# A longer latency for GpSimd's two-column power in the scheduler of a 256-token encoder trunk

## The chip, the cores and the metric

The kernel runs on one core of a Trainium2 chip. The metric is the time of one execution on the device in microseconds (us); of several executions the median is taken. The engines are TensorE (PE for its matmuls, PEld for its weight loads), VectorE (DVE), ScalarE (ACT), GpSimd (POOL) and the queue that issues the transfers (SP).

## What is computed

The trunk has two layers of width 1024 over 256 tokens, in float32. Each layer is a half-step feed-forward block, a mixer, and a second half-step feed-forward block. The mixer of the first layer is recurrent (a causal convolution, then a gated linear recurrence); the mixer of the second is differential attention on keys and values that are built once from the output of the first layer.

```python
def rmsnorm(x, g, eps=EPS):
    y = x * lax.rsqrt(jnp.mean(x * x, axis=-1, keepdims=True) + eps)
    return y * g

def swiglu(h, w_gate, w_up, w_down):
    return (jax.nn.silu(h @ w_gate) * (h @ w_up)) @ w_down

for layer in range(DEPTH):                      # DEPTH = 2
    if layer == N_A_LAYERS:                     # N_A_LAYERS = 1
        k_shared, v_shared = shared_kv(x, ...)
    x = x + 0.5 * swiglu(rmsnorm(x, ffn1_norm[layer]), ...)      # d_ff = 2816
    h = rmsnorm(x, mix_norm[layer])
    x = x + (recurrent_block(h, ...) if layer < N_A_LAYERS else diff_attention(h, k_shared, v_shared, ...))
    x = x + 0.5 * swiglu(rmsnorm(x, ffn2_norm[layer]), ...)
```

## The kernel before, in words

**Layout.** The activations stand transposed: channels on the 128 partitions, the 256 tokens along the row, so x is eight tiles of 128 x 256. Weights come in blocks of 128 x 128, eight to a granule of 128 x 1024. Every float32 weight is split into two parts of a shorter type: ScalarE casts the high part (`whi<-raw`), VectorE subtracts it and keeps the low part (`wlo<-raw,whi`). The activations are split in the same way (`xs` for a normalised input, `b` for a product inside a block). A product is then made of a matmul with the high weights against 512 columns (high and low activations side by side) and one with the low weights against 256 columns (`mm2`), or of three matmuls of 256 columns (`mm3`, in the mixers).

**The norm factor.** A norm's gain is put into `xs` beforehand, its factor per token is applied after the product. `rstd` makes it: two matmuls of the squares against a column of ones (`aux<-ones,acc`), one VectorE instruction (`rv`), a power of -0.5 on the two columns of `rv` by GpSimd (`rt_f`, `rt_mix` or `rt_l`), two VectorE instructions that lay the factor on a diagonal (`w<-ident,rt_f`), one float32 matmul that spreads the diagonal over all rows (`aux<-w,ones`, two records in the trace: "the spread"), and a copy by ScalarE into `rb`. VectorE multiplies the products by `rb` later. `rstd` is called six times: "f10", "f20", "l1" and "f21" for the four feed-forward blocks, "mix0" for the recurrent mixer, and "mix1" for attention, which uses the factor per partition and makes no spread.

**What sets the order.** All operations are first recorded (`Recorder.add`), each with a pitch (how long its engine is taken) and a latency (after how long its result can be used) from the function `cost`. `Recorder.plan` then places them one by one on the five engines: at each step it takes the operation that can start first by these estimates, and among those that can start within 60 ns of each other the one with the longest tail of work behind it. The order found in this way, and the buffer of each tile, are then emitted as they are; on the chip an engine takes its instructions in this order and waits at the head of its queue for what is missing. A later estimate for a result therefore moves whatever waits for it further back in its engine's queue, and other work forward.

**Names in the trace.** All instructions are emitted from line 385 and so carry the line L385; they are told apart by the tiles. `mm` is one of six PSUM banks for products, `aux` one of two for everything else. `w` are working tiles. In the feed-forward blocks `w<-mm,w` adds the two halves of a product, which frees the bank, and `w<-w,rb` applies the norm factor. In the recurrent mixer `rbuf<-mm,rb` frees the bank and applies the factor in one, and the small block products of the gates take `w` (a split activation) and `xk` (their weights).

Of the kernel before, what the change touches and what calls it, by code (L numbers as in the profile page):

```python
# [101 lines left out]
def is_ap(v):  # L102
    return hasattr(v, "tensor") and hasattr(v, "ap")


def width(v):
    n = 1
    for _, c in v.ap[1:]:
        n *= c
    return n  # L110
# [12 lines left out]
def sources(a, k):  # L123
    vals = list(a if "out" in k else a[1:]) + [v for n, v in k.items() if n not in ("out", "accum_out")]
    return [v for v in vals if is_ap(v)]


def cost(op):
    k, out = op.k, op.outs[0] if op.outs else None
    ins = sources(op.a, k)  # L130
    psum = [v for v in ins if v.space == bass.MemoryType.PSUM]
    n = width(out) if out is not None else 1
    if op.eng == "tensor":
        if op.fn == "transpose":
            return 109, 220
        m = width(k["rhs"])
        if k["rhs"].dtype == BF16:
            return m / 2.4 + 3, m / 2.4 + 175
        if k["rhs"].dtype == F32R:
            return 0.4428 * m + 3.3, 0.4428 * m + 165  # L140
        p = 4 * m / 2.4 + 3 if m > 8 else 222
        if k["lhsT"].ap[0][1] <= HD:
            p /= 2
        return p, p + 170
    if op.eng == "scalar":
        if op.fn == "preload_act_table":
            return 1294, 1283
        scalars = is_ap(k.get("scale")) + is_ap(k.get("bias"))
        p = n / 1.2 + (65 if psum else 100) + 83 * scalars
        lat = n / 1.2 + (172 if psum else 195) + 93 * scalars  # L150
        return (p + 93, lat + 200) if len(op.outs) > 1 else (p, lat)
    if op.eng == "vector":
        if op.fn in ("reduce_sum", "reduce_max"):
            n = width(ins[0])
        if op.fn == "tensor_copy":
            return n / 1.92 + 67, n / 1.92 + 155
        if op.fn == "memset":
            return max(15, n / 0.96 - 60), n / 0.96 + 40
        if op.fn == "tensor_tensor_scan":
            return n * 2 / 0.96 + 55, n * 2 / 0.96 + 140  # L160
        rate = 0.96
        if op.fn == "tensor_scalar" and not psum:
            rate = 1.92
        scalar = op.fn in ("tensor_scalar", "scalar_tensor_tensor") and len(ins) > (1 if op.fn == "tensor_scalar" else 2)
        return n / rate + (125 if scalar else 68), n / rate + (210 if scalar else 153)
    if op.eng == "gpsimd":
        if op.fn == "memset":
            return 30, 100
        if k.get("op") == ALU.pow:
            return 300 + 170 * n, 340 + 170 * n  # L170
        return 120 + 2.14 * n, 160 + 2.14 * n
    return 420, 0


class Recorder:
# [16 lines left out]
    def add(self, eng, fn, a, k):  # L192
# [3 lines left out]
        op.outs = [v for v in ([k["out"]] if "out" in k else list(a[:1])) + [k.get("accum_out")] if is_ap(v)]  # L196
        ins = sources(a, k)
        op.pitch, op.lat = cost(op)
        op.port = False
        op.narrow = eng == "tensor" and fn == "matmul" and k["lhsT"].ap[0][1] <= HD  # L200
# [974 lines left out]
```

## Time and profile before

| what | value |
|---|---|
| runs before | 935.24, 938.60, 938.62 us, median 938.60 |
| the profiled execution | 935.45 us, of which the span of its instructions is 933.7 us |
| PE busy | 927.1 us (99%) |
| PEld busy | 823.4 us (88%) |
| DVE busy | 723.1 us (77%) |
| ACT busy | 579.8 us (62%) |
| POOL busy | 34.0 us (4%) |
| granted TensorE clock | full (2.4 GHz) through the span |

The span is the time from the first to the last instruction on the engines; 1.75 us of the execution lie around it. A matmul's end is modelled, so that two matmuls that follow each other closely overlap in the rows; how fast TensorE goes is read from the distance between their starts. In the rows, a bracket with "idle before <- releaser" says how long the engine stood idle before the instruction and what ended that.

By stages: 0 to 195 us is the first feed-forward block (start-up to about 22), 195 to 267 the recurrent mixer, 267 to 462 and 462 to 646 two feed-forward blocks, 646 to 740 keys, queries, values and attention, then the last feed-forward block to 933.7.

### The profile page before, as it was taken

To read this page: it belongs to the slowest core of one execution; us is meant where nothing else is said; L and a number is where in the kernel's file an instruction comes from. 1 tells how busy PE (TensorE), PEld (TensorE's weight loads), DVE (VectorE), ACT (ScalarE), POOL (GpSimd) and SP (SyncE) were. 2 spreads that over 40 slices of the span, in tenths; PEclk is the share of its full clock that TensorE was granted. 3 is DMA by queue.
4 is the path that set the end of the run, shared out by engine and by line. 5 is a ranking of instruction groups with operands and counts; after the bars stand their busy time and mean duration, and the time that the engine had idled before them with its cause. 6 is when DMAs were issued, how large, how long until landed. Compare 5 with 4: busy or idle time off the path is not lost.

```text
span 933.7 us, 14664 instructions
## 1 busy us (share of the span) xinstructions
PE 927.1 (99%) x5586; PEld 823.4 (88%) x5586; DVE 723.1 (77%) x1229; ACT 579.8 (62%) x1040; POOL 34.0 (4%) x42
## 2 busy tenths in 40 slices
PE   8999999999999999999999999999999999999998
PEld 6888888899998888888888888888878988888887
DVE  7898887679898888866688788666997688888651
ACT  7666565569975565655565656555589865655541
POOL 0200000000000000000000000001220000000000
PEclk9999999999999999999999999999999999999999
DMA  9665556543475555555555555555443555555540
GB/s 314 247 210 196 181 183 232 208 145 135 139 264 185 181 184 194 200 189 181 187 180 200 200 181 181 191 201 193 143 147 122 177 180 181 183 192 202 201 155 18
DMA packets 25991, 172.33 MB, mean 185 GB/s; under 512 B 3136, under 2 KB 4288, under 8 KB 5568
## 3 DMA queue, kind: packets, MB, share of 16 engines
q1 hardware_dynamic: 25920, 171.39, 53.2%
q8 instruction: 44, 0.72, 0.3%
q14 instruction: 27, 0.22, 0.1%
HBM read 170.33 MB, written 1.05 MB: 184 GB/s over the span
## 4 chain that ended last, share of the span: by engine, by line
PE 93%; DVE 3%; POOL 1%; DMA 1%; issue 1%; SPq 0%; ACT 0%; DVEq 0%; ACTq 0%; POOLq 0%
PE mm L385 91%; PE aux L385 2%; DVE w L385 1%; DMA raw<-wts 1%; DVE wlo L385 1%; DVE ss L385 0%; SPq L385 0%; POOL facq L385 0%; POOL fac L385 0%; POOL rt_mix L385 0%; POOL rt_f L385 0%; DVE acc L385 0%; ACT w L385 0%; DVE fac L385 0%; DVE xs L385 0%
## 5 line engine op out<-in xcount | busy, mean ns | idle before, releaser
L385 PE MATMUL mm<-xs,whi 128*128 128x512 f32 (+1 forms) x1632 | 530.0, 377 | 1.1 <-DVE xs L385 0.9
L385 DVE TENSOR_TENSOR wlo<-raw,whi 128x1024 fp32r<-128x1024 f32 x318 | 388.4, 1224 | 124.1 <-ACT whi L385 123.6
L385 ACT CAST whi<-raw 128x1024 fp32r<-128x1024 f32 x318 | 333.1, 1051 | 198.3 <-PE mm L385 176.3
L385 PE MATMUL mm<-xs,wlo 128*128 128x256 f32 x1520 | 425.7, 281 | 0.1
L385 PEld LDWEIGHTS mm<-xs,whi 128*128 128x128 f32 x1632 | 298.1, 188 | 59.8 <-ACT acc L385 0.7
L385 PE MATMUL mm<-b,whi 128*128 128x512 f32 (+1 forms) x982 | 292.2, 359 | 0.0
L385 PEld LDWEIGHTS mm<-xs,wlo 128*128 128x128 f32 x1520 | 287.1, 189 | 0.8 <-DVE wlo L385 0.5
L385 PE MATMUL mm<-b,wlo 128*128 128x256 f32 x832 | 233.0, 281 | 0.0
L385 PEld LDWEIGHTS mm<-b,whi 128*128 128x128 f32 x982 | 174.6, 188 | 28.6 <-issue 0.3
L385 PEld LDWEIGHTS mm<-b,wlo 128*128 128x128 f32 x832 | 157.5, 189 | 0.0
L385 ACT ACTIVATE w<-mm 128x256 f32<-128x256 f32 x207 | 79.2, 384 | 110.0 <-PE mm L385 105.2
L385 DVE TENSOR_TENSOR w<-mm,w 128x256 f32<-128x256 f32 x176 | 73.2, 420 | 27.2 <-ACT w L385 27.1
L385 DVE TENSOR_TENSOR w<-w,rb 128x512 f32<-128x512 f32 x88 | 60.4, 689 | 0.4
L385 DVE TENSOR_TENSOR w<-w,w 128x256 f32<-128x256 f32 (+2 forms) x104 | 45.2, 439 | 0.0
L385 PE MATMUL mm<-whi,xk 128*128 128x512 f32 x128 | 41.3, 396 | 0.0
L385 ACT ACTIVATE w<-w 128x256 f32<-128x256 f32 x88 | 36.5, 418 | 5.7 <-DVE w L385 4.9
L385 ACT CAST b<-w 128x256 fp32r<-128x256 f32 x88 | 35.4, 406 | 4.1 <-DVE w L385 4.0
L385 DVE TENSOR_TENSOR b<-w,b 128x256 fp32r<-128x256 f32 x88 | 36.3, 417 | 1.9 <-ACT b L385 1.9
L385 DVE SCALAR_TENSOR_TENSOR xa<-mm,xa 128x256 f32<-128x256 f32 x32 | 13.5, 423 | 26.6 <-PE mm L385 18.6
L385 PEld LDWEIGHTS mm<-whi,xk 128*128 128x128 f32 x128 | 23.8, 188 | 4.6
L385 PE MATMUL mm<-wlo,xk 128*128 128x512 f32 x64 | 25.1, 393 | 0.0
L385 ACT ACTIVATE xs<-xa,vt 128x256 fp32r<-128x256 f32 x40 | 19.5, 502 | 7.3 <-DVE xa L385 7.3
(127 smaller groups left out, 494.0 us busy)
## 6 DMA issues: line engine op xcount, KB each, us to landing
raw<-wts SPq DMA_DIRECT2D x159, 1024.0 KB, 4.8
xa<-head SPq DMA_DIRECT2D x4, 256.0 KB, 5.4
raw<-wts SPq DMA_DIRECT2D x2, 512.0 KB, 7.9
outT<-xa SPq DMA_DIRECT2D x8, 128.0 KB, 2.2
xa<-head SPq DMA_DIRECT2D x2, 384.0 KB, 5.2
rw<-rows SPq DMA_DIRECT2D x1, 320.0 KB, 6.2
xa<-head SPq DMA_DIRECT2D x1, 260.0 KB, 3.6
ident<-eye SPq DMA_DIRECT2D x1, 64.0 KB, 9.9
```

The lines of the kernel that those rows point to most:

```text
L385: getattr(getattr(self.nc, op.eng), op.fn)(*op.a, **op.k)
```

## The change

One constant: the latency that `cost` gives to a power on GpSimd is 900 ns longer where the result has at most two columns (340 + 340 + 900 = 1580 ns instead of 680 ns). No instruction is added or taken away.

```diff
         if k.get("op") == ALU.pow:
-            return 300 + 170 * n, 340 + 170 * n
+            return 300 + 170 * n, 340 + 170 * n + (900 if n <= 2 else 0)
```

Powers on two columns are the six of `rstd` and one in the first block's set-up. GpSimd and SP issue the same rows in the same order as before. TensorE, VectorE and ScalarE have the same instructions in another order at a few places.

TensorE at the first norm factor ("f10"); `mm_152` and `mm_153` are the third column of the gate and up products, `aux_139` is the spread:

```order
 L385 MATMUL mm_153<-xs_0_86,whi_102 128x512
-L385 MATMUL aux_139<-w_7_138,ones_80 128x256
 L385 MATMUL mm_153<-xs_0_86,wlo_103 128x256
 L385 MATMUL mm_152<-xs_0_87,whi_133 128x512
+L385 MATMUL mm_153<-xs_0_87,whi_133 128x512
+L385 MATMUL aux_139<-w_7_138,ones_80 128x256
 L385 MATMUL mm_152<-xs_0_87,wlo_134 128x256
-L385 MATMUL mm_153<-xs_0_87,whi_133 128x512
 L385 MATMUL mm_153<-xs_0_87,wlo_134 128x256
```

The spread stands behind three more matmuls: one of 256 columns and two of 512.

VectorE at the same place; `w_0_141` is the first gate and up product, whose banks `mm_129` and `mm_130` it empties:

```order
 L385 TENSOR_SCALAR rv_136<-aux_135 128x2
 L385 TENSOR_TENSOR wlo_156<-raw_154,whi_155 128x1024
-L385 TENSOR_SCALAR w_7_138<-ident_79,rt_f_0_137 128x128 x2
 L385 TENSOR_TENSOR w_0_141<-mm_129,w_8_142 128x256
 L385 TENSOR_TENSOR w_0_141<-mm_130,w_9_143 128x256
+L385 TENSOR_SCALAR w_7_138<-ident_79,rt_f_0_137 128x128 x2
 L385 TENSOR_TENSOR wlo_158<-raw_154,whi_157 128x1024
```

The two instructions for the diagonal stand behind the two that empty the banks. At "f20", "l1" and "f21" the same happens in small: the diagonal stands behind one such instruction, the spread behind one matmul of 256 and one of 512 columns more. At "mix0" the spread stands behind two more matmuls of 256 columns.

In the recurrent mixer the later factor rearranges the work behind it. The largest move on TensorE is that of the last gate product, `aux_573`, whose input is the split activation `w_5_561`:

```order
 L385 MATMUL mm_578<-xs_0_126,whi_564 128x256 x2
 L385 MATMUL mm_578<-xs_0_126,wlo_565 128x256
+L385 MATMUL aux_573<-w_5_561,xk_459 128x256
 L385 MATMUL mm_578<-xs_0_127,whi_564 128x256 x2
 L385 MATMUL mm_578<-xs_0_127,wlo_565 128x256
-L385 MATMUL mm_578<-xs_0_128,whi_564 128x256 x2
+L385 MATMUL mm_578<-xs_0_128,whi_564 128x256
+L385 MATMUL aux_573<-w_5_561,xk_459 128x256 x5
+L385 MATMUL mm_578<-xs_0_128,whi_564 128x256
 L385 MATMUL mm_578<-xs_0_128,wlo_565 128x256
```

Its first matmul stood behind 7 matmuls of `mm_578` and now stands behind 18; its other five stood behind 11 and now stand behind 22.

ScalarE makes the high part of that activation (`CAST w_5_561`):

```order
 L385 ACT_TABLE_LOAD
-L385 CAST w_5_561<-w_9_560 128x256
 L385 ACTIVATE b_0_494<-b_0_494 128x1024
+L385 CAST w_5_561<-w_4_560 128x256
 L385 ACT_TABLE_LOAD
```

The cast stands behind the square root over 1024 columns, no longer ahead of it.

In attention TensorE and VectorE keep their order. ScalarE, before; `rt_mix_0_1454` is the factor of "mix1", `aux_1464` holds transposed queries:

```order
L385 COPY b_0_1380<-aux_1459 128x4x128
L385 ACTIVATE w_2_1455<-mm_1440,rt_mix_0_1454 128x512
L385 ACTIVATE w_5_1460<-mm_1441,rt_mix_0_1454 128x512
L385 COPY b_0_1380<-aux_1464 128x4x128
L385 CAST whi_1511<-raw_1508 128x1024
```

Now the copy out of `aux_1464` stands ahead of the two squares that need the factor:

```order
L385 COPY b_0_1380<-aux_1459 128x4x128
L385 COPY b_0_1380<-aux_1464 128x4x128
L385 ACTIVATE w_2_1455<-mm_1440,rt_mix_0_1454 128x512
L385 ACTIVATE w_5_1460<-mm_1441,rt_mix_0_1454 128x512
L385 CAST whi_1511<-raw_1508 128x1024
```

At the end of the recurrent mixer some products of its output change places with each other on TensorE, and VectorE adds two output tiles to x ahead of one weight split instead of behind it.

## Rows read from the trace of the kernel before

**Rows 1.** The page, part 1: busy time, share of the span, instructions of each engine.

```profile
PE 927.1 (99%) x5586; PEld 823.4 (88%) x5586; DVE 723.1 (77%) x1229; ACT 579.8 (62%) x1040; POOL 34.0 (4%) x42
```

**Rows 2.** TensorE's waits, all: who waited for whom, total us, times, longest.

```profile
PE aux L385 <- DVE rbuf L385: 1.0, 1, 1.0
PE aux L385 <- DVE w L385: 0.9, 2, 0.5
PE mm L385 <- DVE xs L385: 0.9, 2, 0.5
PE mm L385 <- ACT whi L385: 0.2, 1, 0.2
```

**Rows 3.** Timeline of TensorE at "f10": start, us, instruction, count, idle before.

```profile
20.83 0.40 PE L385 MATMUL mm<-xs,whi 128*128 128x512 f32 x1
21.07 0.28 PE L385 MATMUL mm<-xs,wlo 128*128 128x256 f32 x1
21.18 0.40 PE L385 MATMUL mm<-xs,whi 128*128 128x512 f32 x1
21.99 0.67 PE L385 MATMUL aux<-w,ones 128*128 128x256 f32 x2 [0.41 <-DVE w L385]
```

**Rows 4.** Timeline of VectorE and GpSimd at "f10".

```profile
19.56 1.22 DVE L385 TENSOR_TENSOR wlo<-raw,whi 128x1024 fp32r<-128x1024 f32 x1
...
19.79 1.53 POOL L385 TENSOR_TENSOR rt_f<-rv,mhalf 128x2 f32<-128x2 f32 x1 [18.92 <-DVE rv L385]
...
21.36 0.48 DVE L385 TENSOR_SCALAR w<-ident,rt_f 128x128 f32<-128x128 f32 x2 [0.59 <-POOL rt_f L385]
21.76 0.75 DVE L385 TENSOR_TENSOR w<-mm,w 128x256 f32<-128x256 f32 x2
```

**Rows 5.** Timelines: powers on two columns elsewhere, and VectorE beside one.

```profile
61.39 0.41 DVE L385 TENSOR_TENSOR w<-mm,w 128x256 f32<-128x256 f32 x1
...
61.53 0.69 POOL L385 TENSOR_TENSOR ls<-ebase,ls 128x2 f32<-128x2 f32 x1
...
279.63 0.70 POOL L385 TENSOR_TENSOR rt_f<-rv,mhalf 128x2 f32<-128x2 f32 x1 [81.82 <-DVE rv L385]
```

**Rows 6.** Timeline of VectorE and TensorE at "f20".

```profile
281.14 0.47 DVE L385 TENSOR_SCALAR w<-ident,rt_f 128x128 f32<-128x128 f32 x2
...
281.91 0.59 PE L385 MATMUL aux<-w,ones 128*128 128x256 f32 x2
```

**Rows 7.** Sums of the recurrent stretch: us, then PE, PEld, DVE, ACT, POOL busy (count), clock, DMA, GB/s.

```profile
195.00:245.00 50.00, 50.00 (x418) 49.95 (x417) 46.05 (x95) 43.59 (x78) 0.70 (x1) 1.00 0.43 148
```

**Rows 8.** Timelines of ScalarE and TensorE at the last gate product.

```profile
226.56 0.41 ACT L385 CAST w<-w 128x256 fp32r<-128x256 f32 x1
226.88 1.05 ACT L385 ACTIVATE b<-b 128x1024 f32<-128x1024 f32 x1
...
227.26 0.28 PE L385 MATMUL aux<-w,xk 128*128 128x256 f32 x1
...
227.86 0.76 PE L385 MATMUL aux<-w,xk 128*128 128x256 f32 x5
```

**Rows 9.** Timelines in attention: query transposes, ScalarE's squares, TensorE's wait.

```profile
674.42 0.60 PE L385 MATMUL aux<-ident,w 128*128 128x128 f32 x4
...
676.88 1.26 ACT L385 ACTIVATE w<-mm,rt_mix 128x512 f32<-128x512 f32 x2 [1.87 <-POOL rt_mix L385]
...
684.97 0.63 PE L385 MATMUL aux<-ident,w 128*128 128x128 f32 x4 [0.49 <-DVE w L385]
```

**Rows 10.** Timeline of TensorE ahead of and behind the spread of "f20".

```profile
267.44 0.40 PE L385 MATMUL mm<-xs,whi 128*128 128x512 f32 x1
...
278.76 0.50 PE L385 MATMUL aux<-ones,acc 128*128 128x1 f32 x4
...
282.46 0.39 PE L385 MATMUL mm<-xs,whi 128*128 128x512 f32 x1
...
287.66 0.39 PE L385 MATMUL mm<-xs,whi 128*128 128x512 f32 x1
```

## The prediction

> **What bounds the kernel now.** I read the page's busy times first. TensorE's matmuls cover 99% of the span, at the full clock; no other engine is above 88% [rows 1]. A busy TensorE can hide slack, because matmul ends are modelled, so the second view is the list of TensorE's waits: 3.0 us in six waits [rows 2], of 933.7. Two of the six, 0.9 us together, are of the kind that this change can touch: a matmul into `aux` that waits for VectorE's `w`. The timelines place them: 0.41 us ahead of the spread of "f10" [rows 3] and 0.49 us ahead of a transpose in attention [rows 9]. The other four belong to the start-up. Everywhere else TensorE runs back to back. So only two things can change the time: a wait of TensorE that goes, or one that comes.
>
> The Trainium skill speaks against this reading (Perfetto Trace Analysis, Identifying the Most-Contended Engine): matmul busy time is a poor measure, and the share of weight loading is a good one. By that, with 88% [rows 1], some 110 us would be slack, a wait of half a microsecond could be hidden, and the sum would be 0. The trace decides for the matmuls here: in the feed-forward blocks a 512-column matmul starts and the next follows 0.24 us later, a 256-column one 0.11 us later [rows 3], without a hole; weight loading is at 88% because one load fits twice into the longer matmul.
>
> **The change part by part.** No instruction is added, so all of the cost lies in waits.
>
> *"f10", TensorE.* Before, the 512-column matmul at 21.18 could have been followed at about 21.41 (the one at 20.83 was, after 0.24) and the spread began at 21.99 [rows 3]: 0.58 us lost from start to start, of which the profile calls 0.41 idle. The three matmuls that now stand ahead of the spread take 0.11 + 0.24 + 0.24 = 0.59 us, and their operands were split well before: TensorE gets to the spread at 21.99 or 22.00, with the work of 0.59 us done that it did later before.
>
> *"f10", VectorE.* The weight split ends at 20.78, VectorE then stands idle for 0.59 us, lays the diagonal from 21.36 to 21.84 and empties the banks from 21.76 [rows 4]. Now it empties the banks in the idle time: from 20.70 or 20.78 (instructions overlap by some 0.08), for 0.66 to 0.75 (the two take 0.75, less the overlap), so until 21.36 to 21.53. Its inputs, two tails by ScalarE, are older than that. The diagonal then ends between 21.84 and 22.01, and the spread, which began 0.15 after it before, can begin between 21.99 and 22.16. Left of the wait: 0 to 0.17 us. Gain: 0.58 less that, 0.41 to 0.58. I take **0.5 us**, near the middle; its smaller end is also what one gets from the profile's own figure of 0.41.
>
> That rests on GpSimd's power still ending at 21.32. It took 1.53 us here against 0.70 elsewhere [rows 4, 5] and ended 0.55 after VectorE's split did. Now VectorE goes on with the two bank instructions where it stood idle. One power on two columns that began inside such an instruction took 0.69 [rows 5], so I let it end at 21.32.
>
> *"f20", "l1", "f21".* Before "f20" the diagonal was done at 281.61 and the spread began at 281.91 without a wait [rows 6]; the other two look the same. Now the diagonal comes one bank instruction later (half of the 0.66 to 0.75 us that two take [rows 4], 0.33 to 0.38) and the spread 0.11 + 0.24 = 0.35 us later. The lead of 0.3 us stays: cost 0. `rb` is later by the same 0.35; who waits for it is VectorE's `w<-w,rb`, some microseconds on, which frees no bank: 0.
>
> *"mix0" and the recurrent mixer.* The spread moves by two matmuls of 0.12 us (50.00 us for 418 of them [rows 7]), 0.24 us. There `rb` frees banks and starts the convolution, and VectorE is busy for 46.05 of 50.00 us, so the delay is not simply swallowed; it shifts the chain until VectorE next waits. TensorE's order was drawn up for it: most gate products find their inputs earlier than before. The tightest place is the last one. Its first matmul moves from 227.26 by 11 matmuls, 1.32 us, to 228.58, the other five from 227.86 to 229.18. Its high part moves behind the square root of 1.05 us [rows 8]: its end goes from 226.97 to 228.0, or to 228.3 with the 0.3 us by which ScalarE's queue ahead of it is longer. The lead was 0.29 and is now 0.3 to 0.6 us. (The 0.3 is an estimate from the order and the durations of the rows.) Cost 0; if the lead were gone, TensorE would wait for the rest of such a piece, up to 0.5 us.
>
> *The mixer's output.* The products that change places need the same inputs a few matmuls later than before, and the weight split that is put back by two additions is used only in the next block, which begins at 267.44 [rows 10]. Cost 0.
>
> *Attention.* ScalarE's squares waited 1.87 us for the factor, until 676.88, and the copy that now stands ahead of them has its transposes finished at 675.02 [rows 9]. Some 0.6 us of copying fits: the squares stay at 676.88, the weight cast behind them comes 0.5 us sooner. TensorE's wait of 0.49 at 684.97 hangs on the next pair of query products, which TensorE finishes no earlier: 0.
>
> **The sum**: 935.45 - 0.5 = 934.95 us for an execution like the profiled one. With the bounds: 0.41 to 0.58 gained, up to 0.5 lost in the mixer, so 934.9 to 935.5.
>
> **How this stands to the median.** The four executions shown come in two kinds: 935.24 and 935.45, and 938.60 and 938.62. The trace offers a reason for the step of 3.15. Ahead of the spread of "f20" a pair of matmuls takes (278.76 - 267.44) / 32 = 354 ns, behind it (287.66 - 282.46) / 15 = 347 ns [rows 10]: TensorE leaves the mixers with a slightly longer spacing, and the spread ends that. A block has 352 pairs of the first kind and 176 of the second; some 487 come after the spread, and at 7 ns each a block that kept the longer spacing would cost 3.4 us (an estimate from these rows). So I read the kinds as no block and one block at the longer spacing. Which comes is a matter of the execution, and the median of three was of the second kind; I forecast the same kind, **938.1 us** (938.6 - 0.5).
>
> **The rivals.**
> - *The median falls on the faster kind.* For it: two of the four executions. 934.95, that is 935.0 us.
> - *The bank instructions hold GpSimd up.* They read one operand in PSUM and one in SBUF. If GpSimd had to wait for them as it did for the split, the power would end 0.55 after 21.45, at 22.0; diagonal to 22.5, spread at 22.7 instead of 21.99: a new wait of 0.7 in place of 0.58, so 0.1 us slower than before on the kind, 938.7. Against it: the 0.69 us beside such an instruction [rows 5]. The Trainium skill (SBUF — State Buffer, SBUF: two separate sides) says that VectorE shuts GpSimd out of their shared port when it reads two SBUF operands; these read one. By that rule this rival falls, and the trace agrees, with that one row.
> - *Slower than before: blocks keep the longer spacing.* At "f10" TensorE used to come to a stop ahead of the spread and now hardly does. If it is such a stop, or the place of the spread between two kinds of matmul, that sets the spacing right, the first block can keep the longer one, from 22 us on. One such block more than before on the median: 938.1 + 3.15 = 941.3, 0.3% slower; two more, 944.4. Against it: at "f20" no stop was needed, the spread began without a wait [rows 6] and the spacing changed.
> - *The change doesn't do what it says.* The spread does stand later in the order. But where the power took 0.70 the old constant was right, and there the move wins nothing; only "f10" had a wait to win. If VectorE's two bank instructions waited for a tail that I place too early, the gain is lost: 938.6.
>
> **How the numbers follow.** Forecast, 0.5 gained on the kind of the median: 0.50. The faster kind: 0.30. GpSimd held up, or the gain lost in another way, 938.6 to 939.2: 0.10. Longer spacing in a block more: 0.07, in two more: 0.03. The range goes from 934.4 (the faster kind with 0.6 gained and the 0.4 or so by which runs of a kind differ) to 939.2 and leaves out the last two. Half a percent, 4.7 us, is about what a measurement of this kernel can tell from no change; all but the last case lie within it. Faster by more than that would need 933.9, below every case: 0.02 for what I have not seen. Slower: 0.04. The same: 0.94.
>
> **What would show it.** In the profile after, the spread of "f10" should have an idle time before it of 0 to 0.2 us instead of 0.41, VectorE's bank instructions should start at about 20.7 with no wait for `rt_f` or a short one, and the list of TensorE's waits should be shorter by one. A power at "f10" much longer than 1.53 us speaks for GpSimd held up. New waits of TensorE for `w` between 195 and 245 us would show the mixer's leads to be too short. A pair spacing of 354 ns that goes on behind a spread would show the third rival and the reason for the two kinds. The prediction is wrong if the time leaves the two kinds, near 935 and near 938, altogether.

## The result, and the profile after

The changed kernel takes 946.19 us (median of six runs, 944.3 to 948.1), the kernel before 936.89 us in the runs beside them (935.1 to 938.6). The ratio is 1.010, with a 95% interval of 1.0074 to 1.0125: slower, where the forecast was 938.1 us and no change that can be told. Both kernels come in two kinds of runs: before at 935.2 and 938.5, after at 944.5 and 947.9 (the lower and the upper kind below). The lower kinds are 9.3 us apart, the profiled executions 9.21 (944.66 against 935.45).

The busy times on the page, after:

```profile
PE 936.8 (99%) x5586; PEld 823.1 (87%) x5586; DVE 723.7 (77%) x1229; ACT 576.9 (61%) x1040; POOL 35.6 (4%) x42
```

All of TensorE's waits, after (total us, times, longest):

```profile
PE aux L385 <- DVE rbuf L385: 1.0, 1, 1.0
PE mm L385 <- DVE xs L385: 0.8, 2, 0.5
PE aux L385 <- DVE w L385: 0.5, 1, 0.5
```

No new wait came, and the waits are shorter than in [rows 2]: 2.3 us instead of 3.0. TensorE is busy for 99% again. But the same 5586 matmuls now are "busy" for 936.8 us instead of 927.1 [rows 1], while the weight loads take what they took. The lost time lies inside TensorE's busy time: it goes through the same work at a slower pace. The next view shows where.

Sums of four stretches of 100 us, one well inside each feed-forward block, before (us, PE busy (count), PEld, DVE, ACT, POOL busy, granted clock, DMA share, GB/s):

```profile
50.00:150.00 100.00, 100.00 (x579) 88.19 (x578) 84.03 (x157) 61.74 (x108) 2.33 (x2) 1.00 0.56 191
300.00:400.00 100.00, 100.00 (x579) 88.17 (x578) 80.50 (x126) 59.80 (x109) 0.00 (x0) 1.00 0.55 190
500.00:600.00 100.00, 100.00 (x579) 88.19 (x578) 77.47 (x119) 59.66 (x103) 0.00 (x0) 1.00 0.55 190
800.00:900.00 100.00, 100.00 (x579) 88.19 (x578) 74.57 (x111) 55.70 (x94) 0.00 (x0) 1.00 0.56 194
```

The same stretches, after:

```profile
50.00:150.00 100.00, 100.00 (x579) 87.47 (x578) 83.69 (x155) 61.17 (x108) 2.33 (x2) 1.00 0.55 190
300.00:400.00 100.00, 100.00 (x567) 86.67 (x566) 79.25 (x123) 57.26 (x105) 0.00 (x0) 1.00 0.54 188
500.00:600.00 100.00, 100.00 (x568) 86.76 (x568) 76.87 (x119) 58.89 (x104) 0.00 (x0) 1.00 0.53 185
800.00:900.00 100.00, 100.00 (x568) 86.67 (x567) 75.37 (x115) 55.07 (x96) 0.00 (x0) 1.00 0.55 191
```

The number in the first bracket is what to read: TensorE starts 579 matmuls in 100 us in the first block of either kernel, but 567 or 568 in the other three blocks after, with the full clock and "100.00" busy in all of them. From the matmuls' own starts, a pair of a 512-column and a 256-column one takes 346.7 ns where 579 are counted and 353.3 where it is 567 or 568; a block at the first spacing is called short below, one at the second long. Taken from a matmul to the same matmul in the two traces, the block behind "f20" takes 3.45 us more, that behind "l1" 3.31, that behind "f21" 3.10; the first block takes 0.70 less (0.2 of it in the start-up, ahead of "f10"), the recurrent mixer and the end 0.03 more. The sum is 9.19, the whole difference.

The trace gives starts to the nanosecond. Around the spread of "f20" they are this far apart (worked out from the trace; A is a matmul of 512 columns, b one of 256, S a record of the spread, the number is the time to the next start in ns; the last three rows are of experiments below):

```
before        A232 b118 A240 b120 A236 b114 A233 | S215 S28 b309 A230 b116 A230 b117 A230 b117
after         A241 b120 A236 b113 A232 b118 A234 | S215 S27 b306 A230 b117 A233 b118 A241 b120
1 pair later  A241 b120 A235 b114 A232 b118 A234 | S215 S27 b305 A231 b117 A233 b118 A241 b120
2 pairs later A236 b113 A232 b118 A241 b120 A232 | S215 S28 b306 A230 b117 A233 b118 A241 b120
3 pairs later A233 b117 A241 b120 A236 b113 A234 | S215 S28 b308 A231 b116 A230 b117 A230 b116
```

Ahead of the spread TensorE runs at the longer spacing in all rows, and that spacing is a pattern of three pairs: 232+118, 241+120, 236+113 ns, 1060 ns in all. The spread itself stands between a 512-column matmul and its 256-column partner; its place is named here by the last whole pair ahead (236+113, 236+114 and 235+114 are the same place, read 1 ns apart). Before, it comes behind 236+114, and the next pairs are 230+117: the shorter spacing, 347 ns, which then lasts to the end of the block. After, the spread stands one pair later, behind 232+118, and two pairs on the old pattern is back.

What was forecast for "f10" came true. VectorE, GpSimd and TensorE there, after:

```profile
19.43 1.22 DVE L385 TENSOR_TENSOR wlo<-raw,whi 128x1024 fp32r<-128x1024 f32 x1
20.57 0.75 DVE L385 TENSOR_TENSOR w<-mm,w 128x256 f32<-128x256 f32 x2
21.23 0.48 DVE L385 TENSOR_SCALAR w<-ident,rt_f 128x128 f32<-128x128 f32 x2
...
19.67 1.53 POOL L385 TENSOR_TENSOR rt_f<-rv,mhalf 128x2 f32<-128x2 f32 x1 [18.80 <-DVE rv L385]
...
21.35 0.63 PE L385 MATMUL mm<-xs,whi 128*128 128x512 f32 x2
21.87 0.67 PE L385 MATMUL aux<-w,ones 128*128 128x256 f32 x2
```

VectorE empties the banks where it stood idle before [rows 4], the diagonal follows without a wait, and the spread starts 0.29 us after the second 512-column matmul instead of 0.80 after the one ahead of it [rows 3]: 0.06 us over the usual 0.23 is left of a wait of 0.58.

### The profile page after: what moved, and what is told of

The parts are those of the page before. It is cut to its first block, busy times and chain, and to the rows that moved or that the text cites. A ratio compares the mean times of both kernels' runs of the same rounds, so it can differ in the third digit from the quotient of the medians.

```text
span 942.9 us, 14669 instructions
## 1 busy us (share of the span) xinstructions
PE 936.8 (99%) x5586; PEld 823.1 (87%) x5586; DVE 723.7 (77%) x1229; ACT 576.9 (61%) x1040; POOL 35.6 (4%) x42
## 4 chain that ended last, share of the span: by engine, by line
PE 94%; DVE 3%; POOL 1%; DMA 1%; issue 1%; SPq 0%; ACT 0%; ACTq 0%
PE mm L385 92%; PE aux L385 2%; DVE w L385 1%; DMA raw<-wts 1%; DVE wlo L385 1%; DVE ss L385 0%; POOL fac L385 0%; POOL facq L385 0%; POOL rt_mix L385 0%; SPq L385 0%; ACT w L385 0%; ACT whi L385 0%; DVE fac L385 0%; DVE xa L385 0%; DVE mm L385 0%
## 5 line engine op out<-in xcount | busy, mean ns | idle before, releaser
L385 PE MATMUL mm<-xs,whi 128*128 128x512 f32 (+1 forms) x1632 | 536.3, 382 | 1.0 <-DVE xs L385 0.8
L385 PE MATMUL mm<-b,whi 128*128 128x512 f32 (+1 forms) x982 | 295.7, 363 | 0.0
```

Of the source, the lines that this page charges most:

```text
L385: getattr(getattr(self.nc, op.eng), op.fn)(*op.a, **op.k)
```

## The experiments

Three theories. **Theory 1**: the place of the spread in the pattern of three pairs decides whether the block goes on at 347 or 353 ns a pair; the place behind 236+113, where the kernel before has it, is called the good place. **Theory 2**: something else in the changed order, on VectorE or ScalarE, keeps the spacing long. **Theory 3**: the spread ends the long spacing only if it follows its diagonal closely.

**The spread alone, one, two and three pairs later.** An edit behind the planner moves the spread in TensorE's queue past n matmuls (2, then 4, then 6) and leaves every other queue as it was; `spread` holds the spread's number by the norm's name.

```diff
-        nc.tensor.matmul(out=pb[:, 0:T], lhsT=ones, rhs=diag, start=True, stop=True)
+        nc.spread[name] = nc.tensor.matmul(out=pb[:, 0:T], lhsT=ones, rhs=diag, start=True, stop=True).i
...
+        for name, n in shifts.items():
+            q = queue["tensor"]
+            p = q.index(self.spread[name])
+            q.insert(p + n, q.pop(p))
...
-        return nc.plan()
+        return nc.moved(nc.plan(), {'f20': 2, 'f21': 2})
```

> The kernel before, with the spreads of f20 and f21 one pair of matmuls (512 and 256 columns) later in TensorE's queue, and nothing else changed on any engine. Theory 1 (the place of the spread): at the longer spacing TensorE's starts repeat every three pairs (232+118, 241+120, 236+113 ns), and a spread ends it only behind some of the three. One pair later is where the changed kernel has it, so the blocks of f20 and f21 keep 354 ns a pair behind the spread: 2 x 3.15 us, and 3.15 more if l1 then has no effect either; 941.6 or 944.8 us, or 3.2 more where the first block is long too. Theory 2 (the rest of the changed order, on VectorE and ScalarE, keeps the spacing long): nothing moves, 935.3 or 938.6 us.

> The kernel before, with the spreads of f20 and f21 two pairs later. Theory 1: this is the third of the three places, which neither kernel shows; either outcome fits, the two blocks alike: 935.3 (or 938.6) us if it ends the long spacing, 941.6 or more if not. Theory 3 (a spread ends the long spacing only if it starts at most about 0.3 us after its diagonal is done): the lead grows to 1.0 us, so the blocks stay long: 941.6 us or more.

> The kernel before, with the spreads of f20 and f21 three pairs later. Theory 1: three pairs are one full turn of the pattern, so the spread meets the same place as in the kernel before and both blocks go on at 347 ns a pair: 935.3 or 938.6 us. Theory 3: the lead is 1.35 us, the blocks stay long: 941.6 us or more, as with one pair.

Measured, against 938.0 to 938.9 us of the kernel before on the same chip (16 runs, all of the upper kind): one pair 941.6 to 942.0 us and one run at 945.4; two pairs 941.7 to 942.2; three pairs 935.1 to 935.5 (five runs each). The run at 945.4 is the profiled one; its first block is long too. The stretches of the second, third and fourth block, one pair later:

```profile
300.00:400.00 100.00, 100.00 (x567) 86.77 (x567) 79.36 (x125) 58.51 (x108) 0.00 (x0) 1.00 0.53 184
500.00:600.00 100.00, 100.00 (x579) 88.28 (x578) 78.93 (x122) 60.39 (x105) 0.00 (x0) 1.00 0.54 190
800.00:900.00 100.00, 100.00 (x567) 86.77 (x567) 76.03 (x115) 54.89 (x96) 0.00 (x0) 1.00 0.53 188
```

Two pairs later:

```profile
300.00:400.00 100.00, 100.00 (x567) 86.76 (x567) 79.01 (x124) 57.63 (x106) 0.00 (x0) 1.00 0.55 189
500.00:600.00 100.00, 100.00 (x579) 88.33 (x578) 77.85 (x119) 59.97 (x104) 0.00 (x0) 1.00 0.54 191
800.00:900.00 100.00, 100.00 (x567) 86.86 (x566) 74.58 (x114) 55.19 (x96) 0.00 (x0) 1.00 0.53 188
```

Three pairs later (second and fourth block):

```profile
300.00:400.00 100.00, 100.00 (x579) 88.32 (x578) 80.51 (x126) 59.82 (x109) 0.00 (x0) 1.00 0.55 190
...
800.00:900.00 100.00, 100.00 (x579) 88.29 (x578) 74.61 (x111) 55.70 (x94) 0.00 (x0) 1.00 0.56 194
```

In the second block 567, 567, 579: long, long, short. One step in TensorE's queue alone makes a block long, so nothing else in the changed order is needed for it (against theory 2; whether anything else adds to it is asked below); three steps make it short again, with 1.35 us between the end of the diagonal and the spread instead of 0.29, which ends theory 3. With one pair, "l1" has 579 although its block was entered at the long spacing: its spread, not moved here, stands behind 236+113. With two pairs, "l1" has 579 for another reason: the shorter spacing is there already ahead of its spread, and began at the four one-column matmuls of that norm factor (`aux<-ones,acc`). In this trace they came behind 232+120; wherever else the second, third or fourth feed-forward block was entered at the longer spacing, in this and in the other traces (24 times), they came behind 241+120, and the spacing stayed long. So the spread is not the only matmul that can end the longer spacing, and for these four too the place was different where it ended.

**The changed kernel with the three spreads put back.** The same edit on the changed kernel, with -2 for "f20", "l1" and "f21".

> The changed kernel, with the spreads of f20, l1 and f21 alone put back by one pair in TensorE's queue; VectorE, ScalarE and f10 stay as changed. Theory 1: all three blocks go on at 347 ns: 0.5 us under the kernel before, 934.8 or 938.1 us by the first block. Theory 2: 944.5 or 947.9 us as in the changed kernel. A small wait of up to 0.2 us ahead of each spread may come, since the diagonal stands one instruction later on VectorE; if such a wait alters the phase, the blocks may stay long: 941 to 948 us, with that wait to be seen.

Ten runs: three at 935.4 to 936.0, six at 938.2 to 939.0, one at 941.9, median 938.38, against 944.3 to 948.1 of the changed kernel. In the trace TensorE waits for each of the three diagonals, since these stay one instruction later on VectorE: "f20"'s spread starts 332 ns after the matmul ahead, "l1"'s 345, "f21"'s 370, instead of 233. The profiled execution took 938.45 us, and its four blocks show the first one long and the three others short:

```profile
50.00:150.00 100.00, 100.00 (x568) 86.78 (x567) 81.94 (x152) 59.47 (x106) 2.64 (x2) 1.00 0.54 190
300.00:400.00 100.00, 100.00 (x579) 88.30 (x578) 80.86 (x126) 59.89 (x109) 0.00 (x0) 1.00 0.54 190
500.00:600.00 100.00, 100.00 (x579) 88.33 (x578) 77.91 (x119) 59.88 (x104) 0.00 (x0) 1.00 0.54 191
800.00:900.00 100.00, 100.00 (x579) 88.34 (x578) 75.43 (x113) 56.35 (x96) 0.00 (x0) 1.00 0.55 192
```

So the place of the spreads is what cost the 9 us. The runs scatter over three kinds, the highest of which must have a second long block; whether the waits make the outcome vary is not shown, since the next run finds a block long without one.

**The kernel before once more**, unchanged, for a trace of its upper kind.

> The kernel before, unchanged, for another trace. If its execution is of the longer kind (938.5 us), theory 1 has the whole difference of 3.15 to 3.4 us in the first block: the pairs behind f10's spread stay at 353 ns, those behind f20, l1 and f21 are at 347 ns. A rival (the start-up, the mixers or attention take longer) has equal pairs in all four blocks.

The profiled execution took 938.53 us. The first, second and fourth block:

```profile
50.00:150.00 100.00, 100.00 (x579) 88.15 (x578) 83.57 (x155) 60.86 (x107) 2.59 (x2) 1.00 0.55 190
300.00:400.00 100.00, 100.00 (x579) 88.19 (x578) 80.40 (x126) 59.75 (x109) 0.00 (x0) 1.00 0.55 190
...
800.00:900.00 100.00, 100.00 (x568) 86.73 (x567) 73.46 (x111) 54.78 (x93) 0.00 (x0) 1.00 0.56 192
```

One block is long, and that is the 3.1 us between the kinds. But it is the block of "f21", not the first as I expected. Its spread stands at the good place, behind 236+113, did not wait, and started 237 ns after the matmul ahead of it, where the others at that place took 231 to 234; the block stayed long. So the good place alone does not make a block short in every execution. In the run with three pairs more the first block's code is that of the kernel before, and all five runs were of the lower kind beside 16 of the upper one. So on that chip the upper kind most likely came from "f20" or "f21", the only spreads that differ, which fits this trace.

**The changed kernel with the spreads two pairs later still**, three pairs behind where they were before, so that nothing waits: the same edit with 4 for "f20", "l1" and "f21".

> The changed kernel, with the spreads of f20, l1 and f21 two pairs later still in TensorE's queue (three pairs later than in the kernel before), and nothing else moved. Theory 1: the place is that of the kernel before again, nothing waits, all three blocks run at 347 ns a pair, and f10's gain of 0.5 us is left: 934.8 us, or 938.0 where the first block is long. Theory 2 (the rest of the changed order): 944.5 or 947.9 us. Theory 3 (lead over the diagonal): 944.5 us or more.

Twelve runs: four at 934.5 to 934.7, eight at 937.7 to 938.3. The profiled execution is of the upper kind:

```profile
50.00:150.00 100.00, 100.00 (x567) 86.67 (x567) 82.22 (x152) 59.20 (x105) 2.63 (x2) 1.00 0.55 189
300.00:400.00 100.00, 100.00 (x579) 88.19 (x578) 80.84 (x126) 59.86 (x109) 0.00 (x0) 1.00 0.55 190
500.00:600.00 100.00, 100.00 (x579) 88.15 (x578) 77.76 (x119) 59.87 (x104) 0.00 (x0) 1.00 0.55 191
800.00:900.00 100.00, 100.00 (x579) 88.19 (x578) 74.98 (x113) 56.31 (x96) 0.00 (x0) 1.00 0.56 192
```

All that the change does on VectorE and ScalarE is still in, the three moved blocks are short, and the lower kind lies 0.6 us under the lower kind of the kernel before, about the gain at "f10". Theory 2 is out for the whole of the changed order. Here the long block is the first one.

**Two and two.** All high parts of two products first, then their low parts, on the changed kernel:

```diff
-    def mm2(ps, b, xs, start, stop):
-        wh, wl = wblk(b)
-        nc.tensor.matmul(out=ps, lhsT=wh, rhs=xs, start=start, stop=False)
-        nc.tensor.matmul(out=ps[:, 0, :], lhsT=wl, rhs=xs[:, 0, :], start=False, stop=stop)
+    def mm2(pairs):
+        for ps, b, xs, start, stop in pairs:
+            nc.tensor.matmul(out=ps, lhsT=wblk(b)[0], rhs=xs, start=start, stop=False)
+        for ps, b, xs, start, stop in pairs:
+            nc.tensor.matmul(out=ps[:, 0, :], lhsT=wblk(b)[1], rhs=xs[:, 0, :], start=False, stop=stop)
```

> The changed kernel with its matmuls in another grouping in the four blocks: 512, 512, 256, 256 columns instead of 512, 256, 512, 256; the spreads stay where the scheduler puts them. If the longer spacing belongs to the alternation of a 512-column and a 256-column matmul, there is none here, and four matmuls take 693 ns (the sum of 2 x 227 and 2 x 120 ns that equal neighbours show): 934.6 us in every run, whatever the place of a spread. If it belongs to the mix of the two sizes in any grouping, some blocks are longer again: 938 to 948 us, and more than one kind of run.

Ten runs at 937.3 to 937.7: one kind, as the first half of the expectation had it, but 2.9 us above its 934.6. One of the four stretches, which all have this count:

```profile
300.00:400.00 100.00, 100.00 (x576) 87.28 (x575) 77.97 (x125) 60.30 (x107) 0.00 (x0) 1.00 0.55 190
```

576 lies between 579 and 567. The starts repeat every eight matmuls (233, 236, 116, 112, 233, 231, 113, 119 ns), 1393 ns instead of 1387 for the shorter spacing. So this grouping doesn't reach the sum of what equal neighbours take either, but it has a single spacing: all four stretches have the same count, whatever the places of their spreads.

**A second spread in the first block**, on top of the run with two pairs more:

```diff
+        if name == "f10":
+            pk = psa.tile([P, 512], F32, name="aux")
+            nc.spread["again"] = nc.tensor.matmul(out=pk[:, 0:T], lhsT=ones, rhs=diag, start=True, stop=True).i
...
+        q.insert(q.index(self.spread["f10"]) + 12, self.spread["again"])
```

> As the run with the spreads two pairs later, and in the first block the spread of f10 is made a second time, into a bank that nothing reads: one more float32 matmul in TensorE's queue, behind the fifth 512-column matmul after the first one. Theory 1: where the first spread leaves the long spacing, the starts behind it run 230, 233, 241, 235, 232, so the second meets the 232 and ends it; where the first did end it, the second does no harm. It costs 0.44 us (215 + 28 + 309 + 233 ns instead of 230 + 117): 935.2 us in every run, never 938. If a second one can also start the long spacing, or the first block's kind is not set at f10: some runs at 938.5 us.

Six runs, all at 934.9 to 935.4 us, median 935.25, beside 938.30 of the kernel before (30 runs of both kinds): a ratio of 0.9973 with an interval of 0.9960 to 0.9986. The trace shows both spreads and what lies behind them:

```profile
21.94 0.65 PE L429 MATMUL aux<-w,ones 128*128 128x256 f32 x2
...
23.71 0.40 PE L429 MATMUL mm<-xs,whi 128*128 128x512 f32 x1
23.95 0.28 PE L429 MATMUL mm<-xs,wlo 128*128 128x256 f32 x1
24.06 0.40 PE L429 MATMUL mm<-xs,whi 128*128 128x512 f32 x1
24.30 0.59 PE L429 MATMUL aux<-w,ones 128*128 128x256 f32 x2
24.54 0.47 PE L429 MATMUL mm<-xs,wlo 128*128 128x256 f32 x1
24.85 0.39 PE L429 MATMUL mm<-xs,whi 128*128 128x512 f32 x1
```

The first block of that execution:

```profile
50.00:150.00 100.00, 100.00 (x579) 88.15 (x578) 82.95 (x154) 60.67 (x106) 4.19 (x2) 1.00 0.55 190
```

In nanoseconds, the first spread left the long pattern (235, 232, 241, 235 and 233 for the 512-column matmuls behind it), the second came behind 235+114 and was followed by 230+116. An instruction that computes nothing new, 0.44 us of TensorE's time, took the chance out of the first block in all six runs. In the median it is faster than both kernels, and as fast as the kernel before with three pairs more (935.27, on another chip), which keeps the wait at "f10".

**The constant itself**, at 700 and at 1700 instead of 900 ns:

```diff
-            return 300 + 170 * n, 340 + 170 * n + (900 if n <= 2 else 0)
+            return 300 + 170 * n, 340 + 170 * n + (700 if n <= 2 else 0)
```

> The scheduler's constant raised by 700 instead of 900 ns, nothing else. On TensorE this moves one row only: f10's spread stands two pairs later; f20, l1, f21, mix0 and the mixer keep the order of the kernel before. On VectorE f10's diagonal stands behind two bank-emptying instructions, and on ScalarE one copy in attention changes place. Theory 1: f10's wait of 0.58 us is gone, the blocks of f20 and l1 are short, f10's and f21's are long by chance: 934.7, 938.0 or 941.3 us. Theory 2 (f10 and attention carry the slowdown, not the three other spreads): 944 us or more.

Eleven runs: two at 934.6 and 934.8, nine at 937.5 to 938.8, median 937.87. The gain at "f10" is there in full (the spread starts 232 ns after the matmul ahead, and the page's waits of TensorE lose that row), and "f10" and attention carry none of the slowdown.

> The constant raised by 1700 ns. The scheduler then places the spreads of f20, l1 and f21 three pairs later than in the kernel before (one pair later with 900), f10's five pairs later, and shifts more of the mixer. Theory 1: three pairs are the good place again, and no spread waits: 934.7 us, or 938.0 where the first block is long; up to 0.5 us more if the mixer waits. Theory 4 (the later the norm factor, the slower): 944 us or more.

945.66 us in the median (944.65 to 945.82, five runs): on spacing theory 1 was right, on the time not. Stretches of the first two blocks:

```profile
50.00:150.00 100.00, 100.00 (x579) 88.19 (x578) 83.55 (x155) 61.25 (x108) 2.49 (x2) 1.00 0.56 190
300.00:400.00 100.00, 100.00 (x579) 88.15 (x578) 81.58 (x129) 60.38 (x111) 0.00 (x0) 1.00 0.55 187
```

TensorE's longest wait:

```profile
PE mm L385 <- ACT w L385: 8.2, 1, 8.2
```

All four blocks are short. But in the recurrent mixer a gate product waits 8.2 us for a split activation, which ScalarE reaches only behind eight exponentials and hyperbolic tangents, two weight casts, a square root and three table loads. TensorE and ScalarE at the end of that wait:

```profile
229.31 0.58 PE L385 MATMUL mm<-w,xk 128*128 128x256 f32 x1 [8.22 <-ACT w L385]
...
228.85 0.41 ACT L385 CAST w<-w 128x256 fp32r<-128x256 f32 x1
```

Sums of the two stretches behind the wait (the granted clock is the third number from the end):

```profile
229.30:232.40 3.10, 3.09 (x14) 3.09 (x15) 3.09 (x9) 1.25 (x3) 0.00 (x0) 0.50 0.00 0
232.40:240.00 7.60, 7.60 (x66) 7.60 (x65) 6.21 (x14) 6.37 (x13) 0.00 (x0) 1.00 0.13 19
```

So 900 and 1700 ns end near the same time for reasons that have nothing to do with each other: 9 us of slower pace in the one, 8.2 us of waiting and some 1.3 us at half the clock (14 matmuls 0.21 us apart instead of 0.12) in the other.

## Why the prediction was wrong

*"So only two things can change the time: a wait of TensorE that goes, or one that comes."* This step failed. The waits went from 3.0 to 2.3 us and the time up by 9.2. The pace of back-to-back matmuls is a third thing: three blocks went on at 353.3 instead of 346.7 ns a pair, which is 9.9 us, with no wait at all. I had the numbers for it in the text (354 and 347 ns) when I wrote the sentence. The 0.94 for no change rested on this step.

*"The trace decides for the matmuls here ... without a hole."* No hole is not full pace. The Trainium skill's sentence (Perfetto Trace Analysis, Identifying the Most-Contended Engine), that matmul busy time says little, was borne out by the change itself: busy time rose by 9.7 us for the same 5586 matmuls at an unchanged share of 99%. The other measure, the share of weight loading, went from 88% to 87% and would have told little more. Nor does its remainder show as the slack that I worked out from it: at the shorter spacing the trace of before has loads of 187 to 189 ns that start 117 and 230 ns apart, so the two of a pair cover some 305 of 347 ns, 88%, with TensorE at its faster pace.

*The third rival, blocks that keep the longer spacing.* This is what happened, at 0.07 and 0.03 instead of the bulk of the chance, and in three blocks, which I had not priced; the estimate of 3.15 to 3.4 us for a block was right (3.45, 3.31, 3.10). I placed it at "f10", where a stop goes away; but "f10"'s block was short in the profiled execution, and the three others were long. (In the runs at 947.9 us a fourth block is likely long; none of them was traced.) The argument against it, that at "f20" no stop was needed for the spacing to change [rows 6], was true and answered the wrong question: the spread did it without a stop, but only at one place of three. I had taken [rows 10] as an average over 32 pairs. Listed start by start, the same stretch shows the pattern of three, and that the spread moves by exactly one pair in three blocks is in the order. Whether one step would break it could not be read from the trace of before, since it shows only good places; that it might was a reason for a wide range.

*"The lead of 0.3 us stays: cost 0"* ("f20", "l1", "f21"). True of the wait: none came. Wrong of the cost, for the reason above.

*"f10": a gain of 0.41 to 0.58.* Right. 0.52 of the 0.58 went, and the runs with the other blocks short are 0.6 us under the lower kind of before. GpSimd's power again took 1.53 us and ended 0.55 after VectorE's split, with two bank instructions beside its end: the rival that they hold it up is out.

*The recurrent mixer, its output, attention: 0.* Right for this constant: the mixer took 75.68 us against 75.65, and the wait in attention is 0.5 as before [rows 2]. The lead that I worried about is real, though: at 1700 ns the mixer breaks, by 8.2 us.

*The two kinds as no block and one block at the longer spacing.* Right in kind and size: in each traced run of an upper kind one block more is long. It was that of "f21" in the trace of the kernel before, and the first one in the traces with the spreads put back and with two pairs more.

## What to carry to other kernels

An engine that never waits can still change its pace: count instructions per stretch and list the distances of their starts before calling a move free, and list them one by one, since an average hides a pattern. Where a program runs in two or three kinds of times, find the stretch that differs first; here the kinds differed by one block at 353 instead of 347 ns a pair, and a single extra instruction at the right place ended it in all six runs. And a constant that shifts one thing by a scheduler shifts others by whole steps: 700, 900 and 1700 ns gave the old places, bad places, and good places with a broken mixer.

## What was not expected of the hardware

Alternating matmuls of 512 and 256 columns have two lasting paces on TensorE at the full clock: 346.7 ns a pair (as 230+117 throughout, or as 232+118 and 231+112 in turn, as in the changed kernel's first block) and a pattern of three pairs that takes 1060 ns (353.3 each). In the mixers matmuls of 256 columns alone run at 120 ns, in attention those of 512 columns alone at about 227, which adds up to the shorter pace. At "f20", "l1" and "f21" a float32 spread of two records that came without a wait, while TensorE went at the longer pace, turned it into the shorter behind 236+113 ns in 14 of 15 traced cases, and behind 232+118 or 241+120 in none of 7. The 14 of 15 are no rate for untraced runs: 59 of 76 runs of the kernel before are of its upper kind, so a block stays long in most of them, and on the chip where all 16 were, the argument above puts it at a spread in the good place, whose diagonal was done 0.3 us ahead. Where the spreads stand three pairs later, with the diagonal done about 1 us or more ahead, no run points to a long block there: 16 runs of three kernels are of one kind each, and the fourth kernel's traced upper run has its long block at "f10". Whether the longer lead makes the difference is not shown; no run changed the lead alone. At "f10", where the spread waits or its operand is ready at the last moment, both outcomes came from several places. What the pattern is locked to, why it has three pairs, and why the one traced spread at the good place failed, which began 4 ns later than the others, stays open; no run here tells that.

After TensorE had stood still for 8.2 us (the run with 1700 ns), its granted clock was 0.50, the lower of its two levels, for the first 3.1 us of work, and then full again.
